# HGRN2 in a hybrid transformer block: chunk scores and readout on 32-column tiles of TensorE

## The chip, the cores and the metric

The kernel runs on one core of one Trainium2 chip. The metric is the time of the whole program on the device, in microseconds (us). The kernel before takes 3580.84 us, the median of 3 runs (3575.26 to 3581.83).

## The reference, cut to what matters

The program computes two layers of a trunk over 256 context tokens and 1024 latent tokens. In each layer a normalised input goes through one projection whose columns feed four mixers that stand side by side; the change lies in the third of them, HGRN2, a gated linear recurrence with 4 heads, a 64x64 state per head, and chunks of 32 tokens. It runs forwards and backwards over the tokens, and both results are added.

```python
q_dec = q * jnp.exp(cum)
k_inv = k * jnp.exp(-cum)
att = jnp.where(lower_tri, jnp.einsum('bnthd,bnshd->bnhts', q_dec, k_inv), 0.0)   # scores inside a chunk
o_intra = jnp.einsum('bnhts,bnshv->bnthv', att, v)
kv = jnp.einsum('bnshd,bnshv->bnhdv', k_end, v)                                   # what a chunk adds to the state
def step(state, inp):
    dec, kv_c = inp
    return dec[..., None] * state + kv_c, state
...
o_inter = jnp.einsum('bnthd,bnhdv->bnthv', q_dec, s_prev)                          # what the state before a chunk gives
return (o_intra + o_inter)
```

After that each head's 64 values of a token are normalised by their root mean square and multiplied by a gate (`gate_out`). In the second layer the context tokens need no output, only their final state.

## The kernel before, in words

All arithmetic is in fp32. A plain fp32 matmul stands in the trace as two weight loads and two MATMUL records; the large projections use fp32r operands split in a high and a low part (L509 to L511, one record each).

Tokens come in three blocks: two of 512 latent tokens and one of 256 context tokens. The four heads are worked in two pairs. For a pair the loop of the main function projects the queries, then for each of the two directions and each block the gate input `psfm`, and calls `unit`, and last the output gate, and calls `finish`. In `psfm`, `hgqd`, `hgkp` and `hgsp` the features of two heads lie on the 128 partitions (64 rows each) and the tokens along the row. 24 units are run, 20 of them with an output: 16 of 512 tokens and 4 of 256.

A unit with output does the following. ScalarE and VectorE form the decays and from them `hgqd` (the decayed query), `hgkp` (k_inv) and `hgsp` (k_end). TensorE transposes `hgsp` (L604, `hgtp`) and multiplies it, chunk by chunk, with the values `hgv`, on tiles of 32 rows by 64 columns (L613, `hgkvp`). ScalarE copies the four results into `hgkv` (L614), and VectorE runs the recurrence over chunks as one scan (L621). TensorE forms the scores of 128 tokens against 128 tokens in one matmul per head (L631, `hgat`), of which a mask keeps four diagonal squares of 32 (L633, copy_predicated into `hgatt`, whose rest stays zero). Then the readout `hgop`, with the features on partitions: per 128 tokens and head one matmul with `hgv` as weights over all 128 score columns (L640), and per chunk and head one matmul with the 64x64 state as weights over the chunk's 32 queries (L644). The result is copied (L647, forward) or added (L649, backward) into `hgy`.

`finish` squares `hgy`, sums over each head's rows with a matmul by a block of ones (L664, `hgms`), takes the root, and multiplies.

The order of instructions on each engine is made by the framework's scheduler from dependences and its own costs; each engine works through its list in order. Between the parts of a unit it puts other work on TensorE: the projection of the next block (`psfm`), the S5 mixer (`s5ps`, L414 to L447), and in the first layer a matrix-vector product that makes the modulation vectors (`modps`, L1134, and `modt`, L1143), whose weights `modw` are streamed by DMA through two buffers. The PSUM tiles of HGRN2, S5 and the modulation share five banks; `psfm` has three more.

## Time and profile before

| | |
|---|---|
| median of 3 runs | 3580.84 us (3575.26 to 3581.83) |
| the profiled execution | 3594.48 us, span of its instructions 3592.4 us |
| TensorE busy in the span | 3374.6 us (94%) |
| VectorE, ScalarE, GpSimd busy | 2242.0, 1517.0, 210.5 us |
| mean granted TensorE clock | 0.925 of full speed |

Busy time is the time in which at least one instruction of the engine is on record. Matmuls are pipelined, so TensorE at 94% is not at 94% of its peak; how long a kind of matmul really takes is read from the start of one group to the start of the next. A wait is put down to the engine that released it last.

### The profile page before, as it was taken

How to read it: one execution, taken by the hardware profiler on the slowest of the kernel's cores; microseconds unless marked ns; L12 is line 12 of the kernel's file. 1: busy time of each engine (PE TensorE's matmuls, PEld its weight loads, DVE VectorE, ACT ScalarE, POOL GpSimd, SP SyncE). 2: the span in 40 equal slices, each digit the busy share in tenths (PEclk: the TensorE clock that was granted, in tenths of full speed). 3: DMA queues.
4: the chain of work that ended last, by engine and by line, in shares of the span. 5: the costliest groups of instructions: out<-in, count | busy, mean ns of one | idle time of the engine just before them, and what ended most of it. 6: DMA issues, size and time to landing. Idle time of an engine off the chain costs nothing.

```text
span 3592.4 us, 49905 instructions
## 1 busy us (share of the span) xinstructions
PE 3374.6 (94%) x18452; PEld 2564.5 (71%) x18452; DVE 2242.0 (62%) x4615; ACT 1517.0 (42%) x2804; POOL 210.5 (6%) x165
## 2 busy tenths in 40 slices
PE   7999999899999899999999999898999989999898
PEld 4876766555457777888788887776554668888786
DVE  8764454446746988555487724655566576566676
ACT  4144334334544523333354524655344553333344
POOL 0000000002320000000000000000035100000000
PEclk9998887579999899999999999887699999999999
DMA  6434353312032333222544433222010423333733
GB/s 206 156 128 154 121 168 111 97 41 70 29 116 98 108 109 115 87 93 74 203 160 117 129 105 109 78 85 60 18 45 11 155 98 122 97 106 106 246 97 109
DMA packets 251860, 389.54 MB, mean 108 GB/s; under 512 B 41648, under 2 KB 125840, under 8 KB 250848
## 3 DMA queue, kind: packets, MB, share of 16 engines
q1 hardware_dynamic: 240208, 374.69, 32.2%
q0 software_dynamic: 2192, 8.23, 0.9%
q10 hardware_dynamic: 9216, 3.44, 0.4%
q8 instruction: 145, 2.38, 0.3%
q14 instruction: 99, 0.81, 0.1%
HBM read 283.42 MB, written 102.83 MB: 108 GB/s over the span
## 4 chain that ended last, share of the span: by engine, by line
PE 81%; DVE 10%; ACT 4%; DMA 3%; issue 1%; SPq 0%; ACTq 0%; DVEq 0%
PE fpd L510 4%; PE fpd L511 4%; PE fpd L509 4%; PE fpx L509 4%; PE fpx L510 4%; PE fpx L511 4%; PE psfm L509 3%; PE psfm L511 3%; PE psfm L510 3%; PE mlo L1044 3%; PE fpw L509 2%; PE fpw L511 2%; PE fpw L510 2%; PE hgop L644 2%; PE sws L790 2%; PE pso L509 2%
## 5 line engine op out<-in xcount | busy, mean ns | idle before, releaser
L509 PE MATMUL fpd<-bhr,dhr 128*128 128x512 f32 (+1 forms) x792 | 280.5, 368 | 17.9 <-ACT bhr L515 10.3
L510 PE MATMUL fpd<-blr,dhr 128*128 128x512 f32 (+1 forms) x792 | 291.6, 370 | 2.3 <-DVE blr L518 2.3
L511 PE MATMUL fpd<-bhr,dlr 128*128 128x512 f32 (+1 forms) x792 | 289.1, 367 | 0.0
L509 PE MATMUL psfm<-Hh,wfh 128*128 128x512 f32 (+1 forms) x704 | 269.8, 383 | 1.8 <-ACT hgq L556 1.2
L511 PE MATMUL psfm<-Hh,wfl 128*128 128x512 f32 (+1 forms) x704 | 265.9, 378 | 0.0
L510 PE MATMUL psfm<-Hl,wfh 128*128 128x512 f32 (+1 forms) x704 | 264.7, 376 | 0.0
L509 PE MATMUL fpx<-Th,fh 128*128 128x512 f32 x528 | 208.3, 394 | 25.2 <-ACT fh L515 22.9
L515 ACT CAST fh<-fs 128x512 fp32r<-128x512 f32 x176 | 108.8, 621 | 239.9 <-PE fpc L510 68.8
L510 PE MATMUL fpx<-Tl,fh 128*128 128x512 f32 x528 | 207.7, 393 | 1.8 <-DVE Tl L1290 1.8
L511 PE MATMUL fpx<-Th,fl 128*128 128x512 f32 x528 | 207.3, 393 | 0.0
L515 ACT CAST fh<-fq 128x512 fp32r<-128x512 f32 x160 | 99.1, 621 | 222.1 <-issue 93.5
L509 PEld LDWEIGHTS fpd<-bhr,dhr 128*128 128x128 f32 x792 | 147.4, 190 | 42.8 <-ACT bhr L515 18.3
L518 DVE TENSOR_TENSOR fl<-fq,fh 128x512 fp32r<-128x512 f32 x160 | 109.9, 688 | 106.6 <-ACT fh L515 106.6
L510 PEld LDWEIGHTS fpd<-blr,dhr 128*128 128x128 f32 x792 | 150.0, 189 | 30.6 <-DVE blr L518 5.4
L1014 DVE TENSOR_REDUCE mlmc<-mls 128x1 f32<-128x512 f32 (+1 forms) x200 | 114.3, 590 | 88.1 <-PE mls L1013 87.6
L511 PEld LDWEIGHTS fpd<-bhr,dlr 128*128 128x128 f32 x792 | 150.0, 189 | 24.1 <-issue 0.2
L509 PEld LDWEIGHTS psfm<-Hh,wfh 128*128 128x128 f32 x704 | 137.1, 195 | 36.0 <-issue 12.3
L511 PEld LDWEIGHTS psfm<-Hh,wfl 128*128 128x128 f32 x704 | 136.6, 194 | 29.4 <-issue 9.2
L510 PEld LDWEIGHTS psfm<-Hl,wfh 128*128 128x128 f32 x704 | 137.0, 195 | 26.6 <-issue 7.4
L1040 ACT ACTIVATE mlpt<-mlst 128x512 f32<-128x512 f32 (+1 forms) x168 | 97.5, 585 | 113.9 <-PE mlst L511 107.3
L1077 POOL TENSOR_TENSOR mlac<-mlac,mlpt 128x1024 f32<-128x1024 f32 x56 | 137.5, 2455 | 116.2 <-ACT mlpt L1040 115.5
L518 DVE TENSOR_TENSOR fl<-fs,fh 128x512 fp32r<-128x512 f32 x176 | 120.8, 688 | 29.0 <-ACT fh L515 26.5
(529 smaller groups left out, 8539.1 us busy)
## 6 DMA issues: line engine op xcount, KB each, us to landing
fq<-in_w_up SPq DMA_DIRECT2D x188, 256.0 KB, 2.6
btok<-gd SPq DMA_DIRECT2D x154, 256.0 KB, 2.8
modw<-in_w_mod SPq DMA_DIRECT2D x128, 256.0 KB, 3.7
gd<-fg SPq DMA_DIRECT2D x88, 256.0 KB, 2.1
gd<-fgt SPq DMA_DIRECT2D x66, 256.0 KB, 2.1
mw<-in_w_down SPq DMA_DIRECT2D x66, 256.0 KB, 4.5
mw<-in_w_mod SPq DMA_DIRECT2D x32, 512.0 KB, 6.1
wor<-in_w_out SPq DMA_DIRECT2D x32, 512.0 KB, 3.6
```

Of the source, the lines that this page charges most:

```text
L509: nc.tensor.matmul(ps, wh, xh, start=first and i == 0, stop=False, skip_group_check=read)
L510: nc.tensor.matmul(ps, wh, xl, start=False, stop=False, skip_group_check=read)
L511: nc.tensor.matmul(ps, wl, xh, start=False, stop=last and i == n - 1, skip_group_check=read)
L515: i = g.nc.scalar.copy(hi, src)
L518: (eng or g.nc.vector).tensor_tensor(out=lo, in0=src, in1=hi.bitcast(F32), op=OP.subtract)
L644: nc.tensor.matmul(op[r, ts], before[c][r], qd[r, ts], start=False, stop=c == cl[-1])
L790: nc.tensor.matmul(out, q[r], kl[r, c0:c1], start=False, stop=stop)
L1014: V.tensor_reduce(out=mc[:, qb, j:j + 1], in_=s, axis=AX.X, op=OP.max)
L1040: nc.scalar.activation(out=pt, in_=ps, func=AF.Exp, scale=MLA_SCALE)
L1044: nc.tensor.matmul(po[c], vt[:, b, 64 * h:64 * h + 64], pt[:, e], start=first, stop=last)
L1077: (V if h == 3 and b > 5 else nc.gpsimd).tensor_tensor(out=acc, in0=acc if b > 1 else prev, in1=pt, op=OP.add)
```

## The change: what it does

Three things, all inside `unit` and `finish`.

1. The scores are formed per chunk: 32 keys against 32 queries, so that a chunk's scores lie on the 32 partitions of its keys. A block of 128 tokens takes four matmuls per head (tiles of 64 rows by 32 columns) in place of one of 128x128. They are issued ahead of the transposes, and the mask is a 32-column one. The masked scores have two buffers for each direction, and `hgv` has two buffers in place of one.
2. The readout has the tokens on partitions: `hgatt` (32x32) and `hgqd` (64x32) become the weights, and the values (64 columns) and the state (64 columns, with a step of 17 numbers in memory) the moving operand. Each head has a PSUM tile of its own, so the result is copied or added in two pieces.
3. `finish` transposes the sums back to features on partitions (4 transposes for 512 tokens) and reads them from PSUM.

```diff
-        vt = self.pool.tile([128, 4, 128], F32, name="hgv", bufs=1)[:, 0:m]
+        vt = self.pool.tile([128, 4, 128], F32, name="hgv", bufs=2)[:, 0:m]
...
+        heads = slice(0, 64), slice(64, 128)
+        if need_o:
+            pss = [self.ps(f"at{h}")[:, 0:HC * m].rearrange("p (m t) -> p m t", t=HC) for h in range(2)]
+            for i in range(m):
+                for c in range(4):
+                    ts = slice(i * 128 + c * HC, i * 128 + c * HC + HC)
+                    for r, ps in zip(heads, pss):
+                        nc.tensor.matmul(ps[32 * c:32 * c + 32, i], kp[r, ts], qd[r, ts], start=True, stop=True)
+            at = g.hgatt[d][self.count[d] % 2]
+            self.count[d] += 1
+            for h in range(2):
+                V.copy_predicated(at[:, h, 0:m], g.hgtri[:, d].unsqueeze(1).to_broadcast([128, m, HC]), pss[h])
...
-            for i in range(m):
-                ts = slice(i * 128, i * 128 + 128)
-                nc.tensor.matmul(ps[:, i], kp[r, ts], qd[r, ts], start=True, stop=True)
-            at = g.hgatt[h][d][:, 0:m]
-            V.copy_predicated(at, g.hgtri[:, d].unsqueeze(1).to_broadcast([128, m, 128]), ps)
...
+        ops = [self.ps(f"op{h}")[:, 0:64 * m].rearrange("p (m v) -> p m v", v=64) for h in range(2)]
+        end = [max(c for c in range(j, n, 4) if before[c] is not None) for j in range(4)]
         for i in range(m):
-            cl = [c for c in range(4 * i, 4 * i + 4) if before[c] is not None]
-            for r, at in zip(heads, ats):
-                nc.tensor.matmul(op[r, i * 128:i * 128 + 128], vt[:, i, r], at[:, i], start=True, stop=not cl)
-            for c in cl:
-                ts = slice(c * HC, c * HC + HC)
-                for r in heads:
-                    nc.tensor.matmul(op[r, ts], before[c][r], qd[r, ts], start=False, stop=c == cl[-1])
+            for h, r in enumerate(heads):
+                for c in range(4):
+                    k = slice(32 * c, 32 * c + 32)
+                    nc.tensor.matmul(ops[h][k, i], at[k, h, i], vt[k, i, r], start=i == 0, stop=False)
+        for c in range(n):
+            if before[c] is not None:
+                k = slice(32 * (c % 4), 32 * (c % 4) + 32)
+                for h, r in enumerate(heads):
+                    nc.tensor.matmul(ops[h][k, c // 4], qd[r, c * HC:c * HC + HC], before[c][r], start=False, stop=c == end[c % 4])
...
+        y = self.y[b].rearrange("p (m h v) -> p h m v", h=2, v=64)
+        for h in range(2):
+            if d == 0:
+                nc.scalar.copy(y[:, h], ops[h])
+            else:
+                V.tensor_tensor(out=y[:, h], in0=y[:, h], in1=ops[h], op=OP.add)
...
-        nc.scalar.activation(out=sq, in_=y, func=AF.Square)
+        yt = self.ps("yt")[:, 0:tn]
+        for i in range(0, tn, 128):
+            nc.tensor.transpose(yt[:, i:i + 128], y[:, i:i + 128], g.ident)
+        nc.scalar.activation(out=sq, in_=yt, func=AF.Square)
...
-        V.scalar_tensor_tensor(out=y, in0=y, scalar=ng, in1=sq, op0=OP.mult, op1=OP.mult)
+        V.scalar_tensor_tensor(out=y, in0=yt, scalar=ng, in1=sq, op0=OP.mult, op1=OP.mult)
```

The scheduler sets the order anew. On TensorE, in the first unit of 512 tokens (first layer, first pair of heads, forward), this stands from the state products `hgkvp` to the first readout with a state, before:

```order
L613 MATMUL hgkvp_3481<-hgv,hgkt 64x64 x8
...
L631 MATMUL hgat_3523<-hgqd,hgkp 128x128 x4
L631 MATMUL hgat_3529<-hgqd,hgkp 128x128 x4
L511 MATMUL psfm<-Hh_652,wfl 128x512
L509 MATMUL psfm<-Hh_652,wfh 128x512
L510 MATMUL psfm<-Hl_653,wfh 128x512
L640 MATMUL hgop<-hgatt_2903,hgv 64x128
L445 MATMUL s5ps<-s5RT,s5U 128x128
L446 MATMUL s5ps<-s5RT,s5S 128x128
L640 MATMUL hgop<-hgatt_2905,hgv 64x128
L644 MATMUL hgop<-hgqd,hgkv 64x32 x8
```

and now, from the last scores of that unit on (L608 scores, L617 transposes, L625 state products, L645 and L650 the two readouts):

```order
L608 MATMUL hgat_3501<-hgqd,hgkp 32x32
L617 MATMUL hgtp<-ident,hgsp 128x128 x4
...
L625 MATMUL hgkvp_3573<-hgv,hgkt 64x64 x8
L645 MATMUL hgop_3585<-hgv,hgatt_2904 32x64 x4
...
L445 MATMUL s5ps<-s5RT,s5U 128x128
L446 MATMUL s5ps<-s5RT,s5S 128x128
L447 MATMUL s5ps<-s5RT,s5S 128x128
L445 MATMUL s5ps<-s5RT,s5U 128x128
L446 MATMUL s5ps<-s5RT,s5S 128x128
L650 MATMUL hgop_3585<-hgkv,hgqd 32x64
```

The scores have moved from behind the state products to before the transposes; between the state products and the first matmul that needs the scan there are now the 32 matmuls with the scores and five S5 matmuls.

On ScalarE, in the same unit, the four copies of the state products stand together before (L605 copies the transposes):

```order
L605 COPY hgkt<-hgtp 128x512
L614 COPY hgkv<-hgkvp_3481 128x4x64
L614 COPY hgkv<-hgkvp_3491 128x4x64
L614 COPY hgkv<-hgkvp_3501 128x4x64
L614 COPY hgkv<-hgkvp_3511 128x4x64
L590 ACTIVATE hgdec<-hgcum 128x64x16
L595 ACTIVATE hgkp<-hgsp 128x512
```

and now (L626 are the copies):

```order
L618 COPY hgkt<-hgtp 128x512
L594 ACTIVATE hgqd<-hgcum 128x512
L568 ACTIVATE hglg<-psfm 128x512
L626 COPY hgkv<-hgkvp_3543 128x4x64
L569 ACTIVATE hglg<-hglg 128x512
L626 COPY hgkv<-hgkvp_3553 128x4x64
L595 ACTIVATE hgkp<-hgsp 128x512
L626 COPY hgkv<-hgkvp_3563 128x4x64
L626 COPY hgkv<-hgkvp_3573 128x4x64
```

Two activations that belong to the next block have moved in between the copies of this one, two more ahead of the first copy.

## Rows read from the trace of the kernel before

**Rows 1.** The page: busy time by engine, and the chain by engine.

```profile
PE 3374.6 (94%) x18452; PEld 2564.5 (71%) x18452; DVE 2242.0 (62%) x4615; ACT 1517.0 (42%) x2804; POOL 210.5 (6%) x165
PE 81%; DVE 10%; ACT 4%; DMA 3%; issue 1%; SPq 0%; ACTq 0%; DVEq 0%
```

**Rows 2.** HGRN2's stretch of each layer: length, busy time by engine, granted clock.

```profile
310.00:685.00 375.00, 340.11 (x2945) 247.82 (x2945) 186.58 (x372) 147.04 (x286) 8.02 (x24) 0.79 0.40 123
2250.00:2515.00 265.00, 232.33 (x2079) 183.47 (x2077) 165.56 (x300) 146.69 (x268) 8.23 (x24) 0.82 0.23 69
```

**Rows 3.** Readout tile `hgop`: min/median/max ns; last, waits of its engine (us, times).

```profile
L644 PE MATMUL hgop<-hgqd,hgkv x1136: 272/296/327, 323.9 to 2503.7; 64*64 64x32 f32 x190
L640 PE MATMUL hgop<-hgatt,hgv x288: 272/421/476, 322.8 to 2502.5; 128*64 128x128 f32 x144
...
  DVE hgatt L633: 33.0, 19
```

**Rows 4.** TensorE's timeline, one 512-token unit: start, us, work, records [idle before].

```profile
338.17 1.56 PE L613 MATMUL hgkvp<-hgv,hgkt 32*64 32x64 f32 x64
339.66 1.71 PE L631 MATMUL hgat<-hgqd,hgkp 64*128 64x128 f32 x16
341.30 0.50 PE L511 MATMUL psfm<-Hh,wfl 128*128 128x512 f32 x1
...
344.16 0.40 PE L640 MATMUL hgop<-hgatt,hgv 128*64 128x128 f32 x2 [1.89 <-DVE hgatt L633]
344.50 0.49 PE L445 MATMUL s5ps<-s5RT,s5U 128*128 128x128 f32 x2
...
345.14 0.43 PE L640 MATMUL hgop<-hgatt,hgv 128*64 128x128 f32 x2
...
347.17 1.11 PE L644 MATMUL hgop<-hgqd,hgkv 64*64 64x32 f32 x16
348.20 0.69 PE L640 MATMUL hgop<-hgatt,hgv 128*64 128x128 f32 x4
...
351.53 0.80 PE L447 MATMUL s5ps<-s5RT,s5S 128*128 128x128 f32 x2
```

**Rows 5.** TensorE's timeline: state products of a 256-token unit, full clock.

```profile
319.25 0.53 PE L613 MATMUL hgkvp<-hgv,hgkt 32*64 32x64 f32 x32
319.71 1.19 PE L631 MATMUL hgat<-hgqd,hgkp 64*128 64x128 f32 x8
```

**Rows 6.** TensorE's timeline: state products of a 512-token unit, half clock.

```profile
655.06 2.59 PE L613 MATMUL hgkvp<-hgv,hgkt 32*64 32x64 f32 x64 [0.68 <-ACT hgkt L605]
657.59 2.67 PE L631 MATMUL hgat<-hgqd,hgkp 64*128 64x128 f32 x14
```

**Rows 7.** Timeline of ScalarE and VectorE in the unit of group 4.

```profile
338.90 1.97 ACT L614 COPY hgkv<-hgkvp 128x256 f32<-128x256 f32 x4 [0.96 <-PE hgkvp L613]
340.97 2.42 DVE L621 TENSOR_TENSOR_SCAN hgkv<-hgdec,hgkv 128x1088 f32<-128x1088 f32 x1 [1.33 <-ACT hgkv L614]
343.31 1.33 DVE L633 COPY_PREDICATED hgatt<-hgtri,hgat 128x512 f32<-128x512 uint8 x2
345.33 0.62 ACT L595 ACTIVATE hgkp<-hgsp 128x512 f32<-128x512 f32 x1
```

**Rows 8.** Stretches before and from that unit's readout on; the granted clock is third from last.

```profile
332.10:344.20 12.10, 10.21 (x120) 8.03 (x120) 9.40 (x20) 5.49 (x10) 0.21 (x1) 1.00 0.39 125
345.70:355.90 10.20, 10.20 (x96) 8.92 (x94) 2.23 (x4) 1.78 (x4) 0.21 (x1) 0.50 0.09 27
```

**Rows 9.** Waits of TensorE, second layer's and first layer's stretch: us, times, longest.

```profile
PE hgtp L604 <- ACT hgsp L599: 8.5, 4, 2.7
...
PE modps L1134 <- DMA modw<-in_w_mod: 3.5, 5, 1.1
```

**Rows 10.** TensorE's timeline: four transposes, and the last head norm of layer one.

```profile
336.66 0.66 PE L604 MATMUL hgtp<-ident,hgsp 128*128 128x128 f32 x4
...
680.86 2.07 PE L664 MATMUL hgms<-hglg,ones 128*128 128x512 f32 x2 [3.09 <-ACT hglg L662]
```

More of the change, by code (lines that the diff above doesn't have):

```diff
@@ L550, in start @@
         self.p = p
-        self.q, self.y, self.prev = {}, {}, [None, None]
+        self.q, self.y, self.prev, self.count = {}, {}, [None, None], [0, 0]
     def query(self, b, ps):
@@ L610, in unit @@
             for i in range(m):
-                for h in range(2):
-                    hs = slice(64 * h, 64 * h + 64)
+                for hs in heads:
                     nc.tensor.matmul(ps[hs, i], kt[r, i, hs], vt[r, i, hs], start=True, stop=True)
@@ L681, in hg_consts @@
     nc.vector.memset(g.hgmask[:, 0::HC], 0.0)
-    g.hgatt = [[pool.tile([128, 4, 128], F32, name=f"hgatt{h}{d}") for d in range(2)] for h in range(2)]
-    for h in range(2):
-        for d in range(2):
-            nc.gpsimd.memset(g.hgatt[h][d], 0.0)
-    g.hgtri = pool.tile([128, 2, 128], U8, name="hgtri")
-    t = pool.tile([128, 512], F32, name="hgtrif", tag="hgkp")[:, 0:256].rearrange("p (a b) -> p a b", a=2)
+    g.hgatt = [[pool.tile([128, 2, 4, HC], F32, name=f"hgatt{d}{i}") for i in range(2)] for d in range(2)]
+    for t in (*g.hgatt[0], *g.hgatt[1]):
+        nc.gpsimd.memset(t, 0.0)
+    g.hgtri = pool.tile([128, 2, HC], U8, name="hgtri")
+    t = pool.tile([128, 512], F32, name="hgtrif", tag="hgkp")[:, 0:2 * HC].rearrange("p (a b) -> p a b", a=2)
     nc.sync.dma_start(t, g.io["c_tri"])
@@ L2086, in prep @@
     i = np.arange(128)
-    same = i[:, None] // HC == i[None, :] // HC
-    o["c_tri"] = np.stack([same & (i[:, None] <= i[None, :]), same & (i[:, None] >= i[None, :])], 1).astype(np.float32)
+    j = np.arange(HC)
+    o["c_tri"] = np.stack([i[:, None] % HC <= j[None, :], i[:, None] % HC >= j[None, :]], 1).astype(np.float32)
     neg = np.float32(-1e30)
```

10 lines of the change are left out of this document (removed).

## The prediction, made before the changed kernel was timed

> **What bounds the kernel now.** I read the page's busy times and its chain first. TensorE is busy for 3374.6 us, 94% of the span, and holds 81% of the chain that ended last [rows 1]: time taken off TensorE is, to begin with, time off the kernel. Next I cut out the two stretches in which HGRN2 runs, 375 us and 265 us [rows 2]. TensorE is busy for 340.1 and 232.3 us there, VectorE for 186.6 and 165.6, ScalarE for 147.0 and 146.7. So TensorE bounds both; the other two have room, less of it in the second layer. The clock stands at 0.79 and 0.82 on average there, so much of this is at the lower of its two levels, 1.2 GHz. Then I took the readout tile: 1136 records with a state, 288 with scores, and 33.0 us in 19 waits for the masked scores [rows 3].
>
> I work with one unit of 512 tokens. Its 16 records with scores go into 288 eighteen times, so the kernel holds 18 such units (the 256-token units count half).
>
> **What goes.** From start to start in one unit [rows 4]: the scores take 339.66 to 341.30, that is 1.64 us for 16 records. The readout runs from 344.16 to 351.53, 7.37 us, less 0.64 us of two S5 matmuls in between (344.50 to 345.14): 6.73 us. Together 8.37 us of TensorE. A record with a state costs 1.03 us / 16 = 64 ns there (347.17 to 348.20).
>
> **What comes.** In its place stand three sets of 64 records: scores on tiles of 64 rows by 32 columns, scores times values on 32 by 32, queries times state on 64 by 32. No row has these shapes. The nearest is the state product L613, on tiles of 32 by 64 with 64 moving columns: 64 records in 1.49 us (338.17 to 339.66), 23.3 ns each [rows 4]. As with the new ones, neighbouring matmuls go to other tiles of the array. In the 256-token unit it does 32 records in 0.46 us, 14.4 ns each [rows 5], and at half clock 64 in 2.53 us, 39.5 ns each [rows 6]. The other end is the 64 ns of the old readout, whose two tiles (64 by 64) also lie in the two halves of the rows.
>
> - at 23.3 ns: 192 records take 4.47 us, 3.90 us less per unit, 70 us less in 18
> - at 14.4 ns: 2.76 us, 101 us less in 18
> - at 39.5 ns: 7.58 us, 14 us less
> - at 64 ns: 12.29 us, 3.92 us more, 71 us more
>
> I take 23.3 ns, the row that is nearest in tile size and number of columns, and -70 us.
>
> The Trainium skill (TensorE: Matmul & The Clock Gate, What's actually happening) has a floor of about 25 ns from one matmul's start to the next, however few columns it has. By it 192 records would take 4.8 us, and the gain would be 64 us in place of 70. The trace does not agree: 14.4 ns [rows 5] lies well below.
>
> **What TensorE waits for.** Before, the first readout matmul stands still for 1.89 us because the mask is put on only behind the scan on VectorE: copies 338.90 to 340.87, scan 340.97 to 343.39, two masks from 343.31 [rows 7]. Now the mask is put on early, and that wait goes. What is late next is the scan, for the matmuls with a state. By the order, ScalarE now runs two activations of the next block between the four copies; at 0.62 us each [rows 7] the scan ends at 343.39 + 1.24 = 344.63, 4.97 us after the last state product was issued (339.66). TensorE has in that gap 64 records with scores (1.49 us) and five S5 matmuls at 0.32 us (two took 0.64, [rows 4]), 1.60 us: 3.09 us. It waits for 1.88 us, behind which everything on TensorE stands. That is what it waited before, so this term is 0. Bounds: without the delay on ScalarE the wait is 0.64 us, -22 us in 18 units; if the next block's VectorE work also gets in front of the scan, about another 1.2 us (an estimate: two passes of 0.62 us like those on ScalarE), +22 us.
>
> **What else comes.** `finish` gets 36 transposes (20 in the first layer, 16 in the second). Four take up to 0.66 us [rows 10], and the last ones stand in the chain that closes each layer's stretch, at half clock: I take 5 us, between 4 (36 x 0.1) and 10. The result is taken out in two pieces, on ScalarE and VectorE, which are idle for half of the stretch [rows 2]; behind TensorE it costs nothing, in the closing chain it is inside that 5. The smaller masks (a quarter of the columns) save VectorE time that nobody waits for any more. The second buffer of `hgv` lets a load of values start earlier; no row shows TensorE waiting for that load, so 0.
>
> Then the rest of the work must keep up. TensorE waits 8.5 us for `hgsp` in the second layer and 3.5 us for streamed weights in the first [rows 9]. With some 12% of its 572 us of work gone, more such waits come to light: I take +8 us (from 0 to 24, twice the present 12).
>
> **Sum.** -70 + 0 + 5 + 8 = -57 us. Against the profiled execution: 3594.5 - 57 = 3537.5. The median of the runs stands 13.6 us below the profiled execution; with the same difference the predicted median is 3580.8 - 57 = 3524 us.
>
> **Rivals.**
>
> A. The clock is let go. From 345.7 us, in the middle of that unit's readout, the granted clock is 0.50 for 10.2 us, and just before it was 1.00 [rows 8]; what ran before it fell were the 1.89 us of idle time and the first readout records. Readout ends at 351.53, so some 4.4 us of other work runs at half speed afterwards, 2.2 us of it for nothing; times 18 units 40 us. With a readout half as long the clock might stay up: 3524 - 40 = 3484. Against it: an idle time of the same length stays in front of the readout, and the new matmuls fill no more of the array. So in the main case I leave the clock's cost as it is.
>
> B. The gain turns into waits. ScalarE and VectorE carry a unit's chain, TensorE already waits for `hgsp` [rows 9], and the two activations between the copies show what the scheduler does with freed time. If two thirds of the 57 us are lost to that, 19 us are left: 3562.
>
> C. Slower: column tiles in one half of the rows do not overlap. Scores and state readouts alternate between only two halves of the rows, as the old readout did, at 64 ns a record [rows 4]; the state products at 23.3 ns go over four row groups. If the number of row groups is what counts, scores and state readouts cost 64 ns, the score-times-value matmuls (four row groups) 23.3: 64 x 151.3 ns = 9.68 us, 1.31 us more per unit, +24 us; with the 13 us of the other terms 3618. It decides from a mean of 8.37 us / 192 = 43.6 ns a record on, or 39.8 ns with those 13 us. For it: the strided state is now the moving operand, which no row shows. Against it: the state products use two column halves of each row group, and reach 14.4 ns.
> The Trainium skill (TensorE: Matmul & The Clock Gate, The mechanism) says that a weight load overlaps matmuls in flight only where the row group differs, which is this rival's mechanism; the rates of rows 4 and 5 agree with it as well as with my main case, since their row groups differ.
>
> D. TensorE's busy time falls but nothing moves, within 0.2%: 3581.
>
> **How the numbers follow.** Main case 0.55, own range 3497 to 3553 (the wait's bounds of 22 us and a few us of the others either way); A 0.13; B 0.17; C 0.09; D 0.06. The predicted time is the main case, 3524. The range takes in A with the better bound of the wait (3484 - 22, rounded to 3460) and B with room to D: 3460 to 3578; C and part of D stay out. A measurement of this kernel can tell about 0.2%, 7 us, from no change. Faster by more: main, A and B, 0.85; the same: D, 0.06; slower: C, 0.09.
>
> **What would show it.** The new score and readout records should start 15 to 30 ns apart inside a unit; at 45 or more C holds. The wait for `hgatt` should be gone and one for the scan of about 1.9 us a unit should stand at the first state readout. The two stretches of 375 and 265 us should end up some 30 and 25 us shorter. Clock stretches at 0.50 after each readout should remain; if they are gone, A holds. If TensorE's busy time falls by 60 us or more while its waits for ScalarE and VectorE grow by as much, B holds. Above all a slow strided state as moving operand would make this wrong.

## The result and the profile after

The changed kernel takes 3451.22 us, the median of 4 runs (3446.09 to 3460.3); the kernel before, run beside it, 3578.05 us (3561.79 to 3581.83). The ratio is 0.9659, 95% interval 0.9629 to 0.9688: 127 us less, where 57 had been forecast (3524, range 3460 to 3578). The two profiled executions lie 143.5 us apart in span (3592.4 and 3448.9), 17 us more than the medians, since the one of before was above its median; the accounts below are made between these two.

The page of the changed kernel, busy times and the chain by engine, to be held against [rows 1]:

```profile
PE 3223.9 (93%) x20216; PEld 2457.7 (71%) x20216; DVE 2228.2 (65%) x4625; ACT 1514.7 (44%) x2814; POOL 209.5 (6%) x165
PE 76%; DVE 14%; ACT 4%; DMA 4%; issue 2%; SPq 0%; ACTq 0%; DVEq 0%; POOL 0%; POOLq 0%
```

TensorE lost 150.7 us of busy time though it has 1764 records more. It is still the bound. VectorE's and ScalarE's busy times hardly changed; VectorE's share of the chain went from 10% to 14%.

Where the time went is read best from stretches cut at the same instructions in both traces: HGRN2 of the first layer (first score or transpose to the first `sws` matmul), the attention stage behind it (first `sws` to last `mls` matmul, two tiles of attention scores; the change touches no line of it), and both again in the second layer. Columns: stretch, length, busy us (instructions) of TensorE, its weight loads, VectorE, ScalarE and GpSimd, granted clock, DMA share, GB/s. Before:

```profile
318.20:681.90 363.70, 328.81 (x2877) 239.83 (x2877) 177.14 (x348) 140.60 (x273) 8.02 (x24) 0.79 0.40 123
681.90:993.20 311.30, 296.55 (x1230) 159.46 (x1229) 192.23 (x409) 144.26 (x323) 66.00 (x39) 0.84 0.18 55
2256.70:2511.80 255.10, 223.87 (x2046) 178.49 (x2046) 163.07 (x294) 139.17 (x256) 8.23 (x24) 0.82 0.23 70
2511.80:2772.80 261.00, 249.58 (x1011) 136.56 (x1009) 165.02 (x326) 117.18 (x245) 68.88 (x35) 0.85 0.09 26
```

After:

```profile
318.10:604.70 286.60, 252.84 (x3857) 184.69 (x3857) 168.42 (x354) 137.61 (x279) 8.21 (x24) 0.92 0.51 154
604.70:892.80 288.10, 273.39 (x1230) 147.40 (x1229) 193.87 (x409) 144.72 (x323) 66.16 (x39) 0.93 0.19 60
2159.20:2371.20 212.00, 174.66 (x2830) 140.67 (x2829) 156.54 (x297) 137.82 (x259) 8.26 (x24) 0.91 0.28 84
2371.20:2630.70 259.50, 247.10 (x1010) 135.24 (x1008) 165.49 (x327) 117.85 (x246) 68.94 (x35) 0.86 0.09 25
```

The HGRN2 stretches gave 77.1 and 43.1 us, the first attention stage 23.2, the second 1.5. In the HGRN2 stretches TensorE's busy time fell by 76.0 + 49.2 = 125.2 us, and its idle time (length less busy) rose from 66.1 to 71.1. The first attention stage is the surprise: the same 1230 records took 23.2 us less of TensorE, and its granted clock went from 0.84 to 0.93. How much of that belongs to the change is asked further down.

The records themselves, from the view that groups them (count, busy us and mean ns of one, then idle time before them and what ended it). Before:

```profile
L644 PE MATMUL hgop<-hgqd,hgkv 64*64 64x32 f32 x1136 | 79.2, 295 | 0.0
L640 PE MATMUL hgop<-hgatt,hgv 128*64 128x128 f32 x288 | 53.6, 397 | 32.8 <-DVE hgatt L633 32.7
L631 PE MATMUL hgat<-hgqd,hgkp 64*128 64x128 f32 x288 | 36.0, 307 | 0.1
```

After:

```profile
L625 PE MATMUL hgkvp<-hgv,hgkt 32*64 32x64 f32 x1280 | 31.9, 231 | 1.5 <-ACT hgkt L618 0.7 <-ACT hgkv L626 0.4 <-issue 0.2
L645 PE MATMUL hgop<-hgv,hgatt 32*32 32x64 f32 x1152 | 24.5, 228 | 2.9 <-ACT hgkv L626 1.3 <-issue 0.9 <-DVE hgatt L612 0.6
L650 PE MATMUL hgop<-hgkv,hgqd 64*32 64x64 f32 x1136 | 21.6, 290 | 31.6 <-DVE hgkv L633 30.6 <-issue 0.8
L608 PE MATMUL hgat<-hgqd,hgkp 64*32 64x32 f32 x1152 | 14.6, 203 | 13.7 <-DVE hgqd L596 10.5 <-ACT hgkp L595 3.2
L674 PE MATMUL hgyt<-ident,hgy 128*128 128x128 f32 x36 | 5.9, 278 | 0.0
```

The mean of one record (some 200 to 300 ns) says little here, since records overlap: busy time divided by count gives the pace, 79.2 / 1136 = 69.7 ns before and 21.6 / 1136 = 19.0 ns after for the readout from the state. All busy paces below are such quotients; they count the last record of a run to its end. From start to start, as the expectations have it, they are 1 to 5 ns less (65.4 and 17.5 ns here).

Scores and readouts fell from 168.8 to 60.7 us, the transposes added 5.9: -102.2. So of the 125.2 us, 23.0 are instructions that the change leaves as they were. The account of the pair: records and transposes -102.2, other work in the stretches -23.0, idle time there +5.0, the attention stage -23.2, together -143.4 (the second attention stage and the rest of the program cancel to 0.1).

The unit of [rows 4] in the changed kernel, timeline of TensorE, and last of VectorE (start, us, work, records, idle before):

```profile
329.70 0.76 PE L608 MATMUL hgat<-hgqd,hgkp 64*32 64x32 f32 x64
330.38 0.65 PE L617 MATMUL hgtp<-ident,hgsp 128*128 128x128 f32 x4
...
331.90 1.66 PE L625 MATMUL hgkvp<-hgv,hgkt 32*64 32x64 f32 x64
333.48 1.38 PE L645 MATMUL hgop<-hgv,hgatt 32*32 32x64 f32 x64
334.79 0.49 PE L445 MATMUL s5ps<-s5RT,s5U 128*128 128x128 f32 x2
...
338.12 1.17 PE L650 MATMUL hgop<-hgkv,hgqd 64*32 64x64 f32 x64 [1.95 <-DVE hgkv L633]
339.22 0.79 PE L447 MATMUL s5ps<-s5RT,s5S 128*128 128x128 f32 x2
```

```profile
335.64 2.42 DVE L633 TENSOR_TENSOR_SCAN hgkv<-hgdec,hgkv 128x1088 f32<-128x1088 f32 x1
```

Start to start, the three sets take 0.68, 1.31 and 1.10 us: 10.6, 20.5 and 17.2 ns a record, 3.09 us in place of 8.37. The wait for the scan is there as foreseen: 1.95 us, forecast 1.88; 30.6 us in all, in place of 32.7 for the mask. The single hit has some luck in it: the scan's result came 4.64 us after the last state product (333.48 to 338.12) where 4.97 had been forecast, and TensorE had 2.69 us of work in between where 3.09 had been forecast, so two errors cancel.

### The profile page after: what moved, and what is told of

It is laid out like the page before. It is cut to its first block, busy times and chain, and to the rows that moved or that the text cites. A ratio compares the mean times of both kernels' runs of the same rounds, so it can differ in the third digit from the quotient of the medians.

```text
span 3448.9 us, 53439 instructions
## 1 busy us (share of the span) xinstructions
PE 3223.9 (93%) x20216; PEld 2457.7 (71%) x20216; DVE 2228.2 (65%) x4625; ACT 1514.7 (44%) x2814; POOL 209.5 (6%) x165
## 4 chain that ended last, share of the span: by engine, by line
PE 76%; DVE 14%; ACT 4%; DMA 4%; issue 2%; SPq 0%; ACTq 0%; DVEq 0%; POOL 0%; POOLq 0%
PE fpd L510 5%; PE fpd L511 5%; PE fpd L509 5%; PE fpx L509 4%; PE fpx L510 4%; PE fpx L511 4%; PE mlo L1056 3%; PE psfm L509 3%; PE psfm L510 3%; PE psfm L511 3%; PE fpw L510 2%; PE fpw L511 2%; PE fpw L509 2%; PE pso L511 2%; PE pso L509 2%; PE pso L510 2%
```

## The experiments

"Half clock" is the time in which TensorE was granted the lower of its two levels, worked out from an execution's mean clock c as 2 x (1 - c) x span. Times are medians; each ratio is to runs of the kernel before on the same chip. Half clock is given for the profiled execution and, in brackets, as the median over all executions of the kernel beside these experiments, because the clock differs between executions of one kernel: in 45 of the kernel before it lay between 0.925 and 0.939, and the fastest of them, 3553.66 us, had 0.937, the slowest, 3599.79 us, 0.925. The changed kernel's four had 0.953 to 0.958. The profiled executions of before and e1 lie at the low end of their kernels' clocks, so the brackets compare better. Clock and attention stage are those of the profiled execution alone.

| kernel | us | ratio to before (95%) | clock | half clock, us | first attention stage: us, clock |
|---|---|---|---|---|---|
| before | 3578.05 |  | 0.925 | 539 (486) | 311.3, 0.84 |
| after | 3451.22 | 0.9659 (0.9629 to 0.9688) | 0.955 | 310 (304) | 288.1, 0.93 |
| e1 scores only | 3519.90 | 0.9849 (0.9803 to 0.9894) | 0.935 | 460 (419) | 312.9, 0.85 |
| e2 readout only | 3495.77 | 0.9782 (0.9739 to 0.9825) | 0.950 | 349 (353) | 289.7, 0.92 |
| e3 same tiles | 3475.55 | 0.9725 (0.9684 to 0.9766) | 0.952 | 332 (336) | 286.8, 0.93 |
| e4 contiguous | 3456.88 | 0.9664 (0.9630 to 0.9699) | 0.952 | 331 (328) | 291.1, 0.92 |
| e5 before, contiguous | 3555.57 | 0.9932 (0.9902 to 0.9963) | 0.937 | 448 (448) | 296.0, 0.91 |
| e6 no transposes | 3454.56 | 0.9661 (0.9610 to 0.9713) | 0.955 | 310 (317) | 288.5, 0.93 |
| e7 one buffer | 3445.49 | 0.9635 (0.9608 to 0.9662) | 0.959 | 282 (289) | 288.4, 0.93 |
| e8 split copies | 3458.81 | 0.9654 (0.9613 to 0.9696) | 0.956 | 303 (325) | 289.8, 0.93 |
| e9 state x4 | 3520.91 | 0.9824 (0.9784 to 0.9863) | 0.959 | 288 (296) | 285.8, 0.94 |
| e10 old state too | 3531.43 | 0.9873 (0.9826 to 0.9921) | 0.945 | 388 (392) | 294.8, 0.91 |
| e11 scores late | 3473.43 | 0.9717 (0.9683 to 0.9750) | 0.951 | 340 (344) | 294.0, 0.91 |
| e12 products rotated | 3432.85 | 0.9608 (0.9573 to 0.9643) | 0.964 | 247 (264) | 285.9, 0.94 |
| e13 old score readout too | 3468.57 | 0.9715 (0.9681 to 0.9748) | 0.956 | 305 (302) | 297.4, 0.90 |

### One part at a time (e1, e2)

e1 is the kernel before with the new scores, issued early, and their mask written into the old 128-wide tile; e2 the kernel before with the new readout and the transposes in `finish`:

```diff
 e1
-                nc.tensor.matmul(ps[:, i], kp[r, ts], qd[r, ts], start=True, stop=True)
+                        nc.tensor.matmul(ps[32 * c:32 * c + 32, i], kp[r, ts], qd[r, ts], start=True, stop=True)
 e2
+                    nc.tensor.matmul(ops[h][k, i], ats[h][k, i, k], vt[k, i, r], start=i == 0, stop=False)
...
+                    nc.tensor.matmul(ops[h][k, c // 4], qd[r, c * HC:c * HC + HC], before[c][r], start=False, stop=c == end[c % 4])
```

> The kernel before with part 1 alone: scores per chunk of 32 on 32-column tiles, ahead of the transposes; the masked squares are copied into the 128-wide tiles of before, and readout and head norm are those of before. Theory (matmul shape and number of tiles in use make the gain, term by term): the scores fall from 34.7 to about 13 us of TensorE, the readout stays at 121 us and with it the stretches at half clock (some 240 us in the two HGRN2 stretches), so 20 to 35 us faster than before, about 3550 us. Rival (the early place of scores and mask makes the gain): the waits go, and most of the 127 us are there, under 3500 us.

> The kernel before with parts 2 and 3 alone: readout with tokens on partitions on 32-column tiles, and the transposes in the head norm; scores, masks and their place are those of before. Theory: the readout falls from 121 to about 43 us of TensorE, and the half-clock stretches shrink with it (from 240 us to under 100 in the two HGRN2 stretches), which gives 25 us more in the stretches and perhaps 20 behind the first; about 3470 us. The wait for the masked scores stays at 33 us. Rival (early place of the scores): not below 3530 us.

Against the runs of before beside them (3570.65 us) e1 gave 51 us and e2 75: together 126 of the 127. e1 came out between its theory's 3550 and its rival's 3500, better than forecast; e2 between 3470 and 3530, nearer to its theory but short of it. The early place of scores and mask, e1's rival, has a share in e1's gain:

```profile
L649 PE MATMUL hgop<-hgqd,hgkv 64*64 64x32 f32 x1136 | 79.0, 290 | 21.8 <-DVE hgkv L636 21.8
L645 PE MATMUL hgop<-hgatt,hgv 128*64 128x128 f32 x288 | 41.4, 367 | 1.2 <-ACT hgkv L629 0.9
L609 PE MATMUL hgat<-hgqd,hgkp 64*32 64x32 f32 x1152 | 14.8, 210 | 9.1 <-DVE hgqd L596 7.3 <-ACT hgkp L595 1.8
```

The scores gave 36.0 - 14.8 = 21.2 us; but the wait in the readout fell too, from 32.7 us for the mask to 21.8 for the scan, and the score readout, unchanged in form, from 53.6 to 41.4. In e2 the wait for the mask is still there (32.7 us), and half clock is down to 349 us all the same; in e1 the old readout is still there, and half clock is at 460. By the medians in brackets e2 alone takes away 133 us of half clock and e1 67, of the 182 between before and after. So the low clock goes mostly with the readout, and not with the idle time ahead of it.

### Same tiles, another order (e3)

The changed kernel; the readout from the state takes the chunks column tile by column tile, so that neighbours in time use two tiles in turn and not eight:

```diff
-        for c in range(n):
+        for c in sorted(range(n), key=lambda c: (c % 4, c)):
             if before[c] is not None:
```

> The changed kernel with the state readout in another order: all chunks of one column tile one after the other, so that neighbouring matmuls use only two tiles (one column, two row halves) as in the kernel before. Theory (tiles in use at a time set the pace): a state record goes from 17 ns to 35 or more, 20 us or more on TensorE, and some of the half-clock stretches come back; 3475 us or more. Rival (the pace comes from the shape, few weight columns and a short matmul, whichever tiles follow each other): 17 ns stays, 3451 us.

```profile
L650 PE MATMUL hgop<-hgkv,hgqd 64*32 64x64 f32 x1136 | 42.9, 291 | 34.6 <-DVE hgkv L633 34.5
```

The busy pace doubles, from 19.0 to 42.9 / 1136 = 37.8 ns, 21.3 us more work; the medians differ by 24 us, though the intervals of the two ratios just touch. The work of a record is the same; only who stands next to it in time changed. The Trainium skill (TensorE: Matmul & The Clock Gate, The mechanism) lets a weight load overlap matmuls in flight only where the row group differs. Both orders change the row half with each matmul (two records), so the rule does not tell them apart; the measurement does: with two tiles 37.8 ns, with eight 19.0.

### The step in memory (e4, e5)

e4 is the changed kernel, e5 the kernel before, each with the state read as 64 neighbouring numbers:

```diff
 e4
-                    nc.tensor.matmul(ops[h][k, c // 4], qd[r, c * HC:c * HC + HC], before[c][r], start=False, stop=c == end[c % 4])
+                    nc.tensor.matmul(ops[h][k, c // 4], qd[r, c * HC:c * HC + HC], kvf[r, c * 64:c * 64 + 64], start=False, stop=c == end[c % 4])
 e5
-                    nc.tensor.matmul(op[r, ts], before[c][r], qd[r, ts], start=False, stop=c == cl[-1])
+                    nc.tensor.matmul(op[r, ts], kvf[r, c * 64:c * 64 + 64], qd[r, ts], start=False, stop=c == cl[-1])
```

> The changed kernel with 64 neighbouring numbers of the state tile as moving operand in place of 64 with a step of 17 (the numbers read are then not the state). Theory: the step costs nothing here, 17 ns a record and 3451 us stay. Rival (the step slows the reading): the pace falls to 12 ns or less, 6 us or more on TensorE.

> The kernel before, with the weights of the readout from the state (its line 644) read as 64 neighbouring numbers of the state's buffer and not with a step of 17; the numbers are not the state then. Theory (the 65 ns a record of before come from having only two tiles to alternate between, not from the step): the record falls by no more than the 3.5 ns that the step cost in the kernel after, so 60 to 65 ns, some 68 to 74 us in all, and the time stays within 15 us of before. Rival (the step slows the weight load, and the change gained by making the state the moving operand): the record falls to about 40 ns, half the gain of the state readout, and the time to about 3540.

```profile
L650 PE MATMUL hgop<-hgkv,hgqd 64*32 64x64 f32 x1136 | 17.7, 249 | 33.9 <-DVE hgkv L633 33.2 <-issue 0.7
```

```profile
L644 PE MATMUL hgop<-hgqd,hgkv 64*64 64x32 f32 x1136 | 64.5, 265 | 0.0
```

As moving operand the step costs 19.0 - 15.6 = 3.4 ns a record, more than the theory's nothing and less than the rival's 5, and nothing that can be seen in time. As weights it costs 69.7 - 56.8 = 12.9 ns by busy pace, 14.7 us, where the theory allowed 3.5 ns; the time fell by 21 us, more than the 15 allowed for.

These means mix both clock levels, and for e5 they hide what the step costs. Here are 16 state records and what follows them, from TensorE's timeline: the kernel before at a granted clock of 1.00, e5 at 1.00, and e5 at 0.50 (the kernel before at 0.50 stands in [rows 4]):

```profile
419.54 1.09 PE L644 MATMUL hgop<-hgqd,hgkv 64*64 64x32 f32 x16
420.55 0.47 PE L640 MATMUL hgop<-hgatt,hgv 128*64 128x128 f32 x4
...
612.41 0.65 PE L644 MATMUL hgop<-hgqd,hgkv 64*64 64x32 f32 x16
612.99 0.44 PE L640 MATMUL hgop<-hgatt,hgv 128*64 128x128 f32 x4
...
344.49 1.07 PE L644 MATMUL hgop<-hgqd,hgkv 64*64 64x32 f32 x16
345.48 0.69 PE L640 MATMUL hgop<-hgatt,hgv 128*64 128x128 f32 x4
```

From start to start the kernel before takes 63.1 ns a record at full clock and 64 at half; e5 takes 36.3 at full clock and 61.9 at half. So at full clock the strided weight load was 27 of the 63 ns, and e5's rival (about 40 ns) is right; at half clock it was 2 ns, and the theory is right. The mean looks like the theory because much of e5's readout still ran at half clock. e4 goes the same way: a unit's 64 state records take 0.79 us at full clock (from 337.27) where the changed kernel takes 1.06 (from 394.76), 12.3 ns for 16.6, and 1.11 us for 1.12 at half clock (from 526.34 and 526.92). What is left at full clock, 36 ns, is close to what e3 takes over two tiles (37.8). The old readout was slow for two things, then: the step in its weights, and two tiles in turn.

### What should not matter (e6, e7)

e6 leaves out the transposes in `finish`; e7 has one buffer each for the values and the masked scores:

```diff
 e6
-            nc.tensor.transpose(yt[:, i:i + 128], y[:, i:i + 128], g.ident)
 e7
-        vt = self.pool.tile([128, 4, 128], F32, name="hgv", bufs=2)[:, 0:m]
+        vt = self.pool.tile([128, 4, 128], F32, name="hgv", bufs=1)[:, 0:m]
...
-            at = g.hgatt[d][self.count[d] % 2]
+            at = g.hgatt[d][0]
```

> The changed kernel without the transposes of the sums in the head norm; the norm is taken over the sums as they lie, with tokens on partitions, so the values are not the reference's. Theory (the transposes cost about their own TensorE time, 4.4 us, plus a short wait each): 3 to 12 us faster than the changed kernel, 3440 to 3448. Rival (they stand in a chain that TensorE waits for, and cost several times their own time): 25 us or more faster, below 3426.

> The changed kernel with one buffer in place of two for the values and for the masked scores of each direction. Theory (the extra buffers are not what bought the time): the same as the changed kernel within 7 us, 3444 to 3458. Rival (the values land late, or the masks of the next unit wait for the readout of the last): 20 us more or worse, above 3470.

Both medians are within 6 us of the changed kernel's, and their intervals overlap with its own. Leaving out the 5.9 us of transposes bought nothing that can be seen (3 to 12 us had been expected), and the second buffers bought nothing that can be seen either.

### The wait for the scan (e8, e11)

e8 puts two of the four copies ahead of the scan on VectorE; e11 issues scores behind the state products, masks behind the scan, and the state readout ahead of the score readout:

```diff
 e8
-            nc.scalar.copy(kvv[:, q], ps)
+            (nc.scalar.copy if q % 2 else V.tensor_copy)(kvv[:, q], ps)
 e11
+        if need_o:
+            pss = [self.ps(f"at{h}")[:, 0:HC * m].rearrange("p (m t) -> p m t", t=HC) for h in range(2)]
...
         before = [kv[:, :, c + d] for c in range(n)]
...
+            V.copy_predicated(at[:, h, 0:m], g.hgtri[:, d].unsqueeze(1).to_broadcast([128, m, HC]), pss[h])
...
+                    nc.tensor.matmul(ops[h][k, c // 4], qd[r, c * HC:c * HC + HC], before[c][r], start=c == first4[c % 4], stop=False)
...
+                    nc.tensor.matmul(ops[h][k, i], at[k, h, i], vt[k, i, r], start=False, stop=i == m - 1)
```

> The changed kernel with two of the four copies of the chunk products into the state's buffer on VectorE in place of ScalarE. The scan over the state starts when the last of the four has landed, and TensorE waits 30.6 us in 17 units for it. Theory (the copies on one engine set the start of the scan): the scan starts about 0.6 us earlier a unit, the wait falls to about 20 us, and the time by 10 to 20 us, 3430 to 3441. Rival (VectorE is queued by then with five operations of the next block, so the wait only moves): the same within 7 us.

> The changed kernel with the scores put behind the chunk products instead of ahead of them, their masks behind the scan over the state, and the readout from the state ahead of the readout with the scores. Theory (TensorE waits 30.6 us for the scan in 17 units, and the scores and the readout hide there only as far as they are issued there): the 0.76 us of scores fill a part of the wait, but the 1.4 us of the score readout, which fills it now, moves behind it, so the wait grows by about 0.6 us a unit and the time by about 10 us, 3455 to 3470. Rival (whatever stands in the wait is filled by other matmuls anyway): the same within 7 us.

e8's wait fell to 25.7 us in 15 and not to 20, and the time did not fall: 7.6 us above the changed kernel's, with overlapping intervals, so nearer to the rival. e11's wait did not grow (30.5 us in 18), yet it is 22 us slower, more than either side said; half clock is at 340 us, and other waits came up, for the modulation vectors (`modt` for `modr` 14.5 us against 5.4, `modps` for its streamed weights 7.1 against 1.1 in the first stretch) and `hgtp` for `hgsp` (10.9 against 3.7). Why the new order brings these is not settled. The wait for the scan is real, but to shorten it by 5 us bought nothing.

### The clock: long or slow? (e9, e10, e13)

Three kernels add matmuls behind the readout from the state: e9 the new state readout three times more, e10 the old one once, e13 the old readout with the scores once:

```diff
 e9
+        for _ in range(3):
...
+                        nc.tensor.matmul(ops[h][k, c // 4], qd[r, c * HC:c * HC + HC], before[c][r], start=False, stop=c == end[c % 4], skip_group_check=True)
 e10
+                    nc.tensor.matmul(ops[h][r, c // 4, 0:HC], before[c][r], qd[r, c * HC:c * HC + HC], start=False, stop=c == end[c % 4], skip_group_check=True)
 e13
+                nc.tensor.matmul(ops[h][r, 0:2].rearrange("p m v -> p (m v)"), vt[:, i, r], at[:, h].rearrange("p m t -> p (m t)"), start=False, stop=i == m - 1, skip_group_check=True)
```

> The changed kernel with the matmuls of the readout from the state issued four times over, so that the state's part is counted four times. The added records are 3 x 1136 at 17.5 ns, 60 us. Theory (the clock's gain after the change comes from the small matmuls being so short: TensorE's granted clock falls behind a long stretch of them): half-clock time goes from 310 us back toward the 539 of before, and the time rises by clearly more than the 60 us, to 3540 or above. Rival (the clock follows something else, such as the waits around): the time rises by the 60 us to 3511 within 10, at about 310 us of half clock.

> The changed kernel with the 1136 records of the old readout from the state (64 x 64 of the state as weights, 32 moving columns) issued behind the new one, into the same sums, which are wrong then. In the kernel before they took 65.4 ns each, 74 us. Theory (the slow pace of just these records is what the granted clock fell behind): 74 us more of TensorE work, and on top half-clock time back from 310 to 400 us or more, in the sliding-window stage behind the first stretch too (from 41 us back to above 80 there, and that stage from 288 to about 310 us), so 3545 to 3575. Rival (the clock fell for the whole of the old order: scores, waits and readouts together): 74 us more, half-clock time near 310, 3515 to 3535.

> The changed kernel with the 288 records of the old readout with the scores (128 x 64 weights, 128 moving columns) issued behind the new one, into the same sums, which are wrong then. In the kernel before they took 164 ns each, 47 us, two thirds of it at half clock. Theory (the old readout from the state alone is what the clock fell behind, so these records cost their time at full clock): 110 to 130 ns a record, 32 to 37 us, half-clock time 300 to 325, 3483 to 3492. Rival (these records bring the clock down as well): 140 ns a record or more, half-clock time above 350 us, 3500 to 3525.

The added records of each, from the grouped view:

```profile
L656 PE MATMUL hgop<-hgkv,hgqd 64*32 64x64 f32 x3408 | 60.6, 290 | 21.0 <-issue 21.0
```

```profile
L654 PE MATMUL hgop<-hgqd,hgkv 64*64 64x32 f32 x1136 | 68.4, 292 | 0.0
```

```profile
L653 PE MATMUL hgop<-hgatt,hgv 128*64 128x128 f32 x288 | 25.8, 333 | 0.0
```

e9 and e10 add about the same TensorE time, 60.6 and 68.4 us, but e9 at 17.8 ns a record and e10 at 60.2. With e9 half clock did not rise (288 against 310, by the medians 296 against 304): my theory, that the shortness of the new stretch keeps the clock up, is wrong, and the rival's 3511 within 10 just holds (3521), with 21.0 us of idle time ahead of the added records ("issue") that neither side had. With e10 half clock rose to 388 and the time by 80 us: these records do bring the clock down, but bring back only 78 of the 229 us that the change had taken away, by the medians 88 of 182; the time lies in the rival's range, the half clock nearer to the theory's 400, so neither is right alone. Whether it is their pace, their tile or their strided weights, e10 does not tell. e13 rose by 17 us with half clock unchanged (305): the old score readout, issued in one run, is not what the clock fell behind. These records ran at 25.8 us / 288 = 89.6 ns, faster than the theory's 110, where they took 53.6 / 288 = 186 before, in turn with the others.

Outside HGRN2 the profiled executions of before and after differ most where the first HGRN2 stretch ends and attention starts. Before, the last 57 us of the one and the first 58 us of the other:

```profile
625.00:682.00 57.00, 45.97 (x412) 29.79 (x411) 20.20 (x28) 22.31 (x36) 2.27 (x5) 0.63 0.34 92
682.00:740.00 58.00, 54.32 (x169) 30.28 (x168) 28.12 (x65) 22.58 (x49) 1.36 (x2) 0.50 0.29 86
```

After, the same place:

```profile
550.00:605.00 55.00, 43.21 (x819) 28.82 (x818) 30.48 (x53) 29.21 (x52) 5.07 (x11) 0.93 0.58 158
605.00:663.00 58.00, 54.61 (x228) 31.16 (x226) 32.91 (x81) 26.03 (x59) 1.76 (x3) 0.71 0.35 106
...
590.00:605.00 15.00, 7.50 (x97) 4.89 (x97) 6.89 (x11) 7.76 (x15) 0.00 (x0) 1.00 0.04 15
605.00:612.00 7.00, 4.82 (x12) 2.34 (x11) 5.28 (x10) 4.18 (x9) 0.00 (x0) 0.50 0.36 99
```

In the profiled execution of before, the clock fell with the last units of HGRN2 and stayed at 0.50 through all of the 58 us of attention; after, TensorE got through 228 records there and not 169. But the clock drops at this place in the changed kernel as well: it is 1.00 in the last 15 us of HGRN2, of which TensorE is busy for 7.5, and 0.50 in the first 7 us of attention. So a low clock at the end of HGRN2 is not needed for the drop, and what differs is how long it lasts.

Of the fifteen kernels e1 alone repeats the stage of before (0.85, 312.9 us). The other thirteen take 286 to 297 us at 0.90 or above, and e5 is one of them, which has the whole old readout with only the state contiguous and leaves HGRN2 at much the same clock as before (0.67 in the last 58 us). Before and e1 are also the two whose profiled execution lay well above its kernel's median (3594 against 3578 us, 3540 against 3520). So the 23 us of this stage may be, in part, those two executions and not the change: the kernel before has one profile, and no run here settles it. Which part of the old order lowers the clock in HGRN2 itself (the alternation, the pace of the whole, the strided weights) stays open too.

### The same trick where the change did not use it (e12)

The changed kernel; the chunk products go over all four quarters of the rows in turn (eight tiles), and the four copies follow:

```diff
-        for q in range(4):
-            r = slice(32 * q, 32 * q + 32)
-            ps = self.ps(f"kvp{q}")[:, 0:64 * m].rearrange("p (m v) -> p m v", v=64)
-            for i in range(m):
+        for i in range(m):
+            for q in range(4):
+                r = slice(32 * q, 32 * q + 32)
                 for hs in heads:
-                    nc.tensor.matmul(ps[hs, i], kt[r, i, hs], vt[r, i, hs], start=True, stop=True)
-            nc.scalar.copy(kvv[:, q], ps)
+                    nc.tensor.matmul(pkv[q][hs, i], kt[r, i, hs], vt[r, i, hs], start=True, stop=True)
+        for q in range(4):
+            nc.scalar.copy(kvv[:, q], pkv[q])
```

> The changed kernel with the same trick in a place that the change did not touch: the chunk products (line 625, 1280 records at 23.6 ns, 30.3 us) are issued token block by token block over the four quarters of TensorE's rows, so that neighbours in time use eight tiles in turn and not two; the four copies follow all of them. Theory (the number of tiles that neighbours in time use in turn sets the pace of small matmuls: 11.2 and 17.5 ns over eight in the changed kernel, 36.1 over two): the record falls to 10 to 18 ns, 7 to 17 us less TensorE work, and the time by 5 to 15 us against the changed kernel, 3436 to 3446. Rival (two tiles in different columns are enough here, since these matmuls have 32 rows): 23 to 25 ns, and the time the same or, as the first copy starts later, up to 10 us longer, 3451 to 3461.

```profile
L625 PE MATMUL hgkvp<-hgv,hgkt 32*64 32x64 f32 x1280 | 21.0, 233 | 5.7 <-ACT hgkt L618 3.1 <-DVE hgatt L612 1.8 <-issue 0.7
```

Waits of TensorE in this kernel (us in total, times, longest):

```profile
PE hgop L651 <- DVE hgkv L634: 26.9, 19, 2.1
...
PE hgop L646 <- ACT hgkv L627: 13.8, 17, 2.1
```

The pace fell from 24.9 to 21.0 us / 1280 = 16.4 ns, 10.9 us less work. The score readout now waits 13.8 us for the copies, in place of 1.3 (HGRN2's PSUM tiles share five banks; that this is the cause was not tried), and the median is still 18 us below the changed kernel's; half clock is lower again, 247 us, by the medians 264 against 304. It is the fastest kernel of the study. e12 raises the number of tiles from two to eight and also changes the row quarter with every second matmul, so it does not say which of the two counts; e3, where the row halves alternate in both orders, shows that the number of column tiles does. Its interval (0.9573 to 0.9643) and the changed kernel's (0.9629 to 0.9688) overlap at the ends, so that it beats the changed kernel is likely and not proved; that it beats the kernel before is.

## Why the prediction was wrong

The direction, the bound and the main mechanism (small matmuls on more tiles take less of TensorE) were right; the size was not. 57 us were forecast, 127 came between the medians and 143.4 between the profiled executions. Two terms of the sum failed: the pace of the new records was mis-sized, and the clock's cost was left as it is. By the prediction's steps:

- **What comes: the pace of the new records, mis-sized.** I took 23.3 ns from the state products, the row nearest in shape. The unit shows 16.1 ns on average (3.09 us / 192), so 5.28 us less per unit, 95 us less in 18, where the prediction had 70. Over all units the busy times give 108. e3 and e12 show why the row misled: the state products alternate between two tiles and are slow for their order, not for their shape. In another order the same products run at 16.4 ns. The order of the loops stood in the code: eight matmuls in a row stay in one quarter of the rows, so "the state products at 23.3 ns go over four row groups", and the remark that the row groups of [rows 4] and [rows 5] differ, were wrong readings. My other bound, 14.4 ns, came from the unit of 256 tokens, where the same loop moves on to other rows twice as often; it gave 101 us and was the better guide. The range never took it in: it was built from the wait's bounds, A and B, and with 14.4 ns the main case is 3524 - 31 = 3493, and with A's 40 us on top 3453, beside the 3451 measured.
- **The clock, left as it was: the other step that failed, put at nothing.** I wrote that in the main case "I leave the clock's cost as it is", and gave the clock let go 0.13 as rival A, with 40 us. It was let go in good part: half clock went from 539 to 310 us (by the medians from 486 to 304), unchanged work in the HGRN2 stretches fell by 23.0 us and the attention stage by 23.2. The 143.5 us between the profiled executions are 17 more than the 127 between the medians; if those 17 are the low clock of that one execution of before, about 30 of the 46 us belong to the change (an estimate). Rival A had the mechanism and nearly the sum, with luck, but not the place: half of the 46 lies behind HGRN2, in a stage that I had not looked at. Why the clock was let go is shown only in part: mostly with the readout (e2), some of it with the old state records (e10). My argument against it (the idle time ahead of the readout stays, and the new matmuls fill no more of the array) failed at its first half: the idle time stayed, 1.95 us, and half clock fell all the same; e2 shows it again. Its second half no run tests.
- **The wait: right.** 0 forecast; the scan's 30.6 us took the place of the mask's 32.7, in the single unit with errors of 0.33 and 0.40 us that cancel.
- **finish: right in size.** 5 us forecast, 5.9 us of busy time; e6 shows that the time does not feel them.
- **The rest must keep up: about right.** +8 forecast; TensorE's idle time in the stretches rose by 5.0, with a new wait of 10.5 us for `hgqd` ahead of the scores and less for `hgsp`, 3.7 in place of 8.5 [rows 9].
- **Rival C** (column tiles in one half of the rows do not overlap): refuted. Score and state records alternate between the same two halves and run at 12.7 and 19.0 ns busy pace; go through the column tiles one after the other, as e3 does, and it is 37.8. The strided state, of which the prediction warned, costs 3.4 ns a record as moving operand (e4); as weights, in the old readout, it had cost 27 at full clock (e5), which the prediction did not see.
- **Rivals B and D:** busy time fell by 150.7 us and the span by 143.5, so only 7 us turned into waits.

The miss of 86 us between the profiled executions is, then: 38 from the pace (108 for 70; 13 of it, 108 less 95, is the difference between all units and the one unit that was priced), 46 from work that was not changed, 3 from idle time, less 1 for the transposes. Between the medians the miss is 70, and the part of the unchanged work some 30.

## What to carry to other kernels

Before pricing small matmuls by a row of the trace, read from the loop how many different tiles of the array neighbours in time use; the same record cost 37.8 ns over two tiles and 19.0 over eight, for another order of one loop. Price a record at each level of the granted clock by itself: the mean of e5 hid that contiguous weights bring the old record from 63 to 36 ns at full clock. Before a difference in the granted clock is put down to a change, hold it against the spread between executions of one kernel: here one execution's draw may account for 17 of 143 us. An idle time that one expects to bring the clock down is best tried by itself: here it stayed and the clock came back.

## What the runs showed of the hardware

- fp32 records on 64 x 32 tiles with 32 columns start 10.6 ns apart at full clock (64 in 0.68 us), the fastest pace seen here; the readout over the four tiles on the diagonal, 32 x 32 with 64 columns, takes 20.5 ns.
- A moving operand with a step of 17 numbers costs 3.4 ns a record over a contiguous one (e4, by busy pace; 4 ns at full clock, next to nothing at half); in a weight load of 64 by 64 the same step costs 27 ns at full clock (16 records in 1.01 us, contiguous in 0.58) and 2 ns at half clock (1.03 and 0.99).
- Matmuls of 17.8 ns, in runs four times as long, leave the granted clock where it was (0.959 against 0.955); matmuls of 60.2 ns for about the same total time bring it to 0.945 (by the medians of four executions each 0.958, 0.956 and 0.945).
- A stage that follows a stretch at full clock can start at half: in the changed kernel the clock was 1.00 in the last 15 us of HGRN2 and 0.50 in the first 7 us of attention. In the kernel before it stayed at 0.50 for the first 58 us of the same stage, whose last 193 us (800 to 993) ran at 0.96.
- The mean clock of one program differs between executions (0.925 to 0.939 in 45 of the kernel before), and its time with it (3599.79 to 3553.66 us).
